# Pilot means behind part of the next tile, the last attention output unit split ahead, and Hyena splits behind the spectrum products

## The chip, the core and the metric

The kernel runs on one NeuronCore of one Trainium2 chip. The number that is compared is the device time of one launch in microseconds (us), the median of several runs. A core has engines that run side by side, each with its own queue of instructions: TensorE (PE, matrix products into the banks of PSUM), VectorE (DVE), ScalarE (ACT), GpSimd (POOL), and SyncE (SP), which issues the DMA transfers. They wait for each other through semaphores. TensorE works at one of two clock levels, 1.2 and 2.4 GHz; the profile gives the granted clock as a share of the higher one.

## What is computed

A backbone of two layers on 256 latent tokens of 1024 features, with 256 context tokens that only layer 0's first half-step and its attention read. Each layer is a half-step SwiGLU, a token mixer and another half-step SwiGLU. Layer 0's mixer is differential attention, layer 1's is a Hyena long convolution. Each of the six sub-layers is modulated by the conditioning and followed by a layer norm over the residual:

```python
def half_ffn(x, shift, scale, gate, wi, wo, g, b, alpha):
    y = swiglu(modulate(x, shift, scale), wi, wo)       # (silu(a) * u) @ wo, a and u from h @ wi
    return layer_norm(alpha * x + 0.5 * gate * y, g, b)

def bidir_long_conv(u, h_f, h_b, d_skip):
    ...
    uf = jnp.fft.rfft(u.astype(jnp.float32), n=n, axis=1)
    hf = jnp.fft.rfft(h_full, n=n, axis=0)
    y = jnp.fft.irfft(uf * hf[None], n=n, axis=1)[:, :L]
    return (y + u.astype(jnp.float32) * d_skip.astype(jnp.float32)).astype(u.dtype)

# layer i:
xl = half_ffn(xl, ml[0], ml[1], ml[2], ffa_wi[i], ffa_wo[i], ln_g[i, 0], ln_b[i, 0], alpha)
# mixer: diff_attention (i = 0) or hyena (i = 1), which is (x0 * bidir_long_conv(x1 * v, h_f, h_b, d_skip)) @ w_o
xl = layer_norm(alpha * xl + ml[5] * yl, ln_g[i, 1], ln_b[i, 1])
xl = half_ffn(xl, ml[6], ml[7], ml[8], ffb_wi[i], ffb_wo[i], ln_g[i, 2], ln_b[i, 2], alpha)
```

All of it is fp32. The FFT is done as products with tables.

## The kernel before

**Tiles.** Activations lie with features on the 128 partitions: eight tiles R[0] to R[7] of 128x256 for the latent tokens (named zl in the trace), and in the first, wide stage eight tiles Z of 128x512 (z) for latent and context together. An fp32 product is made of three products of high and low parts, so each weight is split: ScalarE casts the loaded weight (raw) to its high part (wH, line 237), and VectorE subtracts that from raw to get the low part (wL, line 238).

**Weights.** A queue `st` (class Stream) brings units of up to 1 MB in the order of use. Two raw buffers hold loaded units, three buffers hold split ones. `st.get` takes the next split unit, `st.done` gives its buffer back, and in the same call the next loaded unit's split is issued, and the next load. `st.spare(1)` allows one further unit to be split into four 512-column blocks (xwH, xwL) while the three buffers are taken; `st.spare(0)` ends that.

**Stages, in time.** The wide feed-forward (`ffn_wide`), attention over four pairs of heads with its output in four weight units of two tiles each (`Project`), three feed-forward stages (`ffn`, layer 0's second, layer 1's first, and, after Hyena, layer 1's second), and Hyena. A feed-forward stage's output has eight tiles j; tile j takes two weight units h = 0, 1 of 11 blocks each, a 512-column and a 256-column product per block, into one PSUM bank py. Then scalar_tensor_tensor on VectorE adds gate times py into R[j] (line 885 in the wide stage, 1202 in Project, 1255 in ffn).

**The norm and its pilot.** `Norm` takes the statistics while the output is still made. As soon as tile 0 is added, `pilot` makes the mean of tile 0 over its features on TensorE (lnpm, line 334 through the helper mm), and VectorE subtracts it from all eight tiles (line 735). This keeps the sums small. `add` takes the square on ScalarE and running sums on VectorE for each further tile, and `finish` closes the norm.

**Hyena.** `ramp` runs 12 units n of input weights, the first two interleaved; a unit is 48 products of 256 columns into a bank pxv. Behind unit n, `end` does the short convolution on ScalarE and VectorE (the product of both parts is pkeep), transposes tile n - 2 (ptr, then the halves pTh and pTl), and behind n = 6 and n = 10 (SPECTRUM) calls `spectrum`: products with a table into banks uf, and on VectorE 13 products and sums with the filter's spectrum (lines 1327 to 1334), whose halves yh and yl ScalarE and GpSimd make. After unit 11 follow the inverse transform (yt, 96 products) and a Project with four units.

**Order.** The code names instructions with priorities; a scheduler puts each engine's instructions into one fixed order, by priority and data dependencies. An engine runs its own list in that order. `tc.high_priority` moves what stands in it ahead, `tc.issue_after` puts instructions behind a given one. Splits are issued with a lowered priority. The lines that the change touches are tile_done and pilot, the loops over j in the three kinds of output, the last round (t == 3) of attention, and ramp and spectrum.

## Time and profile before

| | |
|---|---|
| median of 3 runs | 1368.24 us (1368.17 to 1372.35) |
| profiled execution | 1370.3 us, of which the span is 1368.1 |
| mean granted clock of TensorE | 0.976 |
| busy: TensorE, VectorE, ScalarE, GpSimd | 1312.9 us (96%), 1037.2 (76%), 660.0 (48%), 12.3 (1%) |
| DMA | 261.38 MB, mean 191 GB/s |

Times in rows are microseconds from the start of the span. A row of a timeline has start, duration, engine, line, operation, output<-inputs, and in square brackets how long the engine stood idle before it and what ended that. TensorE's products are pipelined, so the distance of two starts is what one costs, not the duration in its row. A product that is written x2 stands for two in a row. A row of windows has the stretch, its length, and then the busy time (with the number of instructions) of TensorE, its weight loads, VectorE, ScalarE and GpSimd, the granted clock, the DMA share and GB/s. In the profiled execution the wide output's second half runs around 360 to 390, attention's output ends at 628, the pilots of the three later feed-forward stages stand at 769, 967 and 1301, and Hyena's spectrum products around 1087 and, the second group, after unit 10.

### The profile page before, as it was taken

The numbers are of one execution on the slowest core, as the hardware profiler recorded it, in microseconds if no ns is written. First come the engines' busy times: TensorE is split into PE (matmuls) and PEld (weight loads), VectorE is DVE, ScalarE is ACT, GpSimd is POOL, SyncE is SP. The second block draws the span as 40 slices with busy tenths as digits, with TensorE's granted clock in tenths as the row PEclk, the third lists the DMA queues.
The fourth block names the chain that finished last, engine by engine and source line by source line (L and its number), as shares of the span: only waits on it lengthen the run. The fifth ranks groups of instructions, "written<-read, shape, count | busy, mean of one in ns | idle before, by whom it ended". The sixth has DMA issues, their size and how long they took to land.

```text
span 1368.1 us, 19280 instructions
## 1 busy us (share of the span) xinstructions
PE 1312.9 (96%) x7424; PEld 1129.7 (83%) x7424; DVE 1037.2 (76%) x1919; ACT 660.0 (48%) x1175; POOL 12.3 (1%) x12
## 2 busy tenths in 40 slices
PE   7999999999999999998999999999999889999997
PEld 4688888888788788887888888888899889888886
DVE  3899988889876777768777667766668789766665
ACT  1443322222233866655765446655446354666543
POOL 0000000000000000000000000000000020000000
PEclk9999999999999999998999999999999999999998
DMA  8967788878842212203654454554563523355452
GB/s 283 398 243 262 275 331 335 331 310 333 309 142 77 93 63 92 93 32 101 216 204 169 160 198 146 197 187 170 194 213 141 192 101 124 126 185 191 160 180 84
DMA packets 44419, 261.38 MB, mean 191 GB/s; under 512 B 4965, under 2 KB 6693, under 8 KB 19625
## 3 DMA queue, kind: packets, MB, share of 16 engines
q1 hardware_dynamic: 44328, 260.16, 53.0%
q8 instruction: 58, 0.95, 0.3%
q14 instruction: 33, 0.26, 0.1%
HBM read 256.99 MB, written 3.15 MB: 190 GB/s over the span
## 4 chain that ended last, share of the span: by engine, by line
PE 84%; DVE 9%; ACT 4%; issue 2%; DMA 1%; ACTq 0%; SPq 0%; DVEq 0%
PE py L334 24%; PE pa L334 22%; PE pu L334 22%; PE pxv L334 5%; PE pv L334 2%; DVE wL L238 1%; ACT wH L237 1%; PE hsp L334 1%; PE pka L334 1%; PE pkb L334 1%; PE warm L334 1%; DMA raw<-wia 1%; PE lnst L334 1%; PE po L334 1%; ACT rsw L925 1%
## 5 line engine op out<-in xcount | busy, mean ns | idle before, releaser
L238 DVE TENSOR_TENSOR wL<-raw,wH 128x1024 fp32r<-128x1024 f32 (+1 forms) x358 | 389.9, 1108 | 119.6 <-ACT wH L237 116.9
L237 ACT CAST wH<-raw 128x1024 fp32r<-128x1024 f32 (+1 forms) x358 | 331.0, 956 | 217.4 <-PE py L334 122.6
L334 PE MATMUL pa<-xhl,wH 128*128 128x512 f32 x520 | 188.2, 399 | 5.6 <-DVE xhl L811 5.6
L334 PE MATMUL py<-g,wH 128*128 128x512 f32 (+1 forms) x594 | 188.1, 374 | 0.0
L334 PE MATMUL pu<-xhl,wH 128*128 128x512 f32 x520 | 187.9, 398 | 0.0
L489 DVE SCALAR_TENSOR_TENSOR rawa<-rawa,condb 128x1024 f32<-128x1024 f32 x128 | 151.2, 1220 | 3.5 <-DMA rawa<-adr 3.3
L334 PE MATMUL py<-g,wL 128*128 128x256 f32 x528 | 148.9, 282 | 0.0
L334 PE MATMUL pa<-xhl,wL 128*128 128x256 f32 x520 | 146.5, 282 | 0.0
L334 PE MATMUL pu<-xhl,wL 128*128 128x256 f32 x520 | 146.3, 281 | 0.0
L334 PEld LDWEIGHTS py<-g,wH 128*128 128x128 f32 x594 | 107.9, 189 | 21.0
L334 PEld LDWEIGHTS pa<-xhl,wH 128*128 128x128 f32 x520 | 98.6, 190 | 29.3 <-DVE xhl L811 4.1
L334 PEld LDWEIGHTS pu<-xhl,wH 128*128 128x128 f32 x520 | 98.7, 190 | 23.2
L334 PEld LDWEIGHTS py<-g,wL 128*128 128x128 f32 x528 | 100.6, 191 | 0.1
L334 PEld LDWEIGHTS pa<-xhl,wL 128*128 128x128 f32 x520 | 99.2, 191 | 0.1
L334 PEld LDWEIGHTS pu<-xhl,wL 128*128 128x128 f32 x520 | 99.3, 191 | 0.0
L841 ACT ACTIVATE sil<-pa 128x512 f32<-128x512 f32 x22 | 13.2, 598 | 152.6 <-PE pa L334 152.6
L334 PE MATMUL pxv<-xhl,wH 128*128 128x256 f32 x384 | 75.5, 298 | 5.2 <-DVE pTl L508 3.8
L334 PEld LDWEIGHTS pxv<-xhl,wH 128*128 128x128 f32 x384 | 64.4, 205 | 5.9 <-DVE pTl L508 4.1
L334 PE MATMUL pa<-xh,wH 128*128 128x512 f32 x176 | 68.6, 390 | 0.0
L334 PE MATMUL pa<-xh,wL 128*128 128x512 f32 x176 | 68.5, 389 | 0.0
L334 PE MATMUL pu<-xh,wH 128*128 128x512 f32 x176 | 68.5, 389 | 0.0
L334 PE MATMUL pu<-xh,wL 128*128 128x512 f32 x176 | 68.5, 389 | 0.0
(314 smaller groups left out, 2601.2 us busy)
## 6 DMA issues: line engine op xcount, KB each, us to landing
rawa<-adr SPq DMA_DIRECT2D x64, 1024.0 KB, 6.9
raw<-wia SPq DMA_DIRECT2D x44, 1024.0 KB, 4.8
raw<-wib SPq DMA_DIRECT2D x44, 1024.0 KB, 4.8
raw<-woa SPq DMA_DIRECT2D x32, 704.0 KB, 4.1
raw<-wob SPq DMA_DIRECT2D x32, 704.0 KB, 4.1
rawa<-adx SPq DMA_DIRECT2D x8, 1024.0 KB, 10.1
raw<-wqk SPq DMA_DIRECT2D x8, 1024.0 KB, 4.7
raw<-whv SPq DMA_DIRECT2D x8, 1024.0 KB, 4.7
```

Of the source, the lines that this page charges most:

```text
L237: nc.scalar.copy(h[:, d], it["raw"][:, s:e])
L238: nc.vector.tensor_tensor(lo[:, d], it["raw"][:, s:e], h[:, d].bitcast(F32), OP.subtract)
L334: return nc.tensor.matmul(o, l, r, start=start, stop=stop, skip_group_check=True)
L489: V.scalar_tensor_tensor(junk if q else w, w, 1.0, condb[:, q, :], OP.mult, OP.mult, accum_out=mod[i][:, q, 2 * u + h:2 * u + h + 1])
L841: S.activation(s, pa, AF.Silu)
L925: S.copy(s3[32 * b:32 * b + 32], ps[32 * (b ^ 1):32 * (b ^ 1) + 32])
```

## The change

Three edits.

(a) The pilot moves. `tile_done` and `pilot` take an instruction `after`, and the pilot's product is issued behind it. In the wide stage it comes behind the first ES = 5 of 11 blocks (15 of 33 products) of tile 1, in ffn behind tile 1's first unit (22 products), in Project behind part of tile 2's products, where tile 0 and tile 1 are both reported. The eight subtracts follow the pilot.

(b) In attention's last round `st.spare(1)` stands ahead of the round and `st.spare(0)` behind it, so one of the output's weight units may be split into blocks.

(c) In Hyena, for n = 6 and n = 10, `end` (convolution, transposition, spectrum) runs first, and `st.done`, with the split that it issues, is put behind the last VectorE instruction of the spectrum products, which are now in a function `product` of their own, unchanged.

```diff
@@ -719,18 +719,20 @@
         def __init__(self, z, n):
             self.z, self.n = z, n
 
-        def tile_done(self, j):
+        def tile_done(self, j, after=None):
 
             with tc.high_priority(120):
                 if j == 0:
-                    self.pilot()
+                    self.pilot(after)
                 if j < KT - 1:
                     self.add(j)
 
-        def pilot(self):
+        def pilot(self, after):
+
             z, n = self.z, self.n
             ps = bank("lnpm")[:, :n]
-            mm(ps, opil, z[0], True, True)
+            with tc.issue_after(after.ins):
+                mm(ps, opil, z[0], True, True)
             for t in range(KT):
                 V.tensor_tensor(z[t], z[t], ps, OP.subtract)
 
@@ -876,6 +878,8 @@
                 mid = gemm(o, G, NH, 0, ES)
                 if half == 1 and j == KT - 1:
                     nrm.early(mid)
+                if half == 1 and j == 1:
+                    nrm.tile_done(0, mid)
                 gemm(o, G, NH, ES)
                 st.done(it, half == 1 and j == KT - 1)
                 wide_side(100 + 50 * half + j)
@@ -884,7 +888,7 @@
                         c = slice(T * q, T * q + T)
                         pin(V.scalar_tensor_tensor(Z[j][:, c], py[:, c], g[:, q, j:j + 1], Z[j][:, c], OP.mult,
                                                    OP.add), j if half else 0)
-                if half == 1:
+                if half == 1 and j:
                     nrm.tile_done(j)
         return nrm
 
@@ -1154,6 +1158,7 @@
                 main = v
             else:
                 pj = Project(O, gate_cols(0, 5, 1, False))
+                st.spare(1)
 
                 def pj_parts():
                     pj.open(2)
@@ -1165,6 +1170,7 @@
 
                 thread(main, PLAN_LAST, now)
                 thread(pj_parts(), PLAN_LAST, now, KT)
+                st.spare(0)
         return pj.close(6)
 
     class Project:
@@ -1195,13 +1201,17 @@
                     mid = gemm(outs[o:o + 1], self.O, KT, k0, ks) if ks > k0 else None
                     if j == KT - 1:
                         self.nrm.early(mid)
-                    gemm(outs[o:o + 1], self.O, KT, ks)
+                    last = gemm(outs[o:o + 1], self.O, KT, ks)
+                    if j == 2:
+                        self.nrm.tile_done(0, mid or last)
+                        self.nrm.tile_done(1)
                     if o:
                         st.done(it, j == KT - 1)
                     with tc.high_priority(PJP):
                         pin(V.scalar_tensor_tensor(R[j], py[:, T * o:T * o + T], self.gt[:, 0, j:j + 1], R[j],
                                                    OP.mult, OP.add), j)
-                    self.nrm.tile_done(j)
+                    if j > 1:
+                        self.nrm.tile_done(j)
                 self.jj += 1
             return self.nrm
 
@@ -1249,15 +1259,19 @@
                     mid = mm(py[:, :T], wl, g[:, :T], False, last)
                 if j == KT - 1 and h == 0:
                     nrm.early(mid)
+                if j == 1 and h == 0:
+                    nrm.tile_done(0, mid)
                 st.done(it, j == KT - 1 and h == 1)
             with tc.high_priority(PJP):
                 for n in range(1 if alone else 2):
                     pin(V.scalar_tensor_tensor(R[j], py[:, T * n:T * n + T], gt[:, 0, j:j + 1], R[j], OP.mult, OP.add), j)
             ada_side(ADA_FFN[s + str(i)].count(NF + j))
-            nrm.tile_done(j)
+            if j:
+                nrm.tile_done(j)
         return nrm
 
-    def ramp(unit, gemm, X, end, n, first=2, ks=5):
+    def ramp(unit, gemm, X, end, n, late=(), first=2, ks=5):
+
 
         grp = [unit() for _ in range(first)]
         gemm([o for g in grp for o in g[2]], X, KT, 0, ks)
@@ -1268,8 +1282,12 @@
             else:
                 it, pp, outs = unit()
                 gemm(outs, X, KT)
-            st.done(it)
-            end(pp, f)
+            if f in late:
+                with tc.issue_after(end(pp, f).ins):
+                    st.done(it)
+            else:
+                st.done(it)
+                end(pp, f)
 
 
     def split_table(src, name):
@@ -1322,21 +1340,27 @@
                         mm(ps, au[tt][0][:, c], lo, False, False)
                         mm(ps, au[tt][1][:, c], h, False, tt == 1)
                     U[ft] = ps
-                ur, ui, hr, hi = U[f], U[2 + f], sp[f, dh], sp[2 + f, dh]
-                yr, yi, t1, t2 = blk("yr"), blk("yi"), blk("yt1"), blk("yt2")
-                V.tensor_tensor(yr, ur, hr, OP.mult)
-                V.tensor_tensor(t1, ui, hi, OP.mult)
-                V.tensor_tensor(yr, yr, t1, OP.subtract)
-                V.tensor_tensor(yi, ur, hi, OP.mult)
-                V.tensor_tensor(t2, ui, hr, OP.mult)
-                V.tensor_tensor(yi, yi, t2, OP.add)
-                if f == 0:
-                    V.tensor_tensor(yi[0:1, :], ui[0:1, :], nyq[dh][0:1, :], OP.mult)
-                for ft, y in ((f, yr), (2 + f, yi)):
-                    h, lo = blk("yh", F32R), blk("yl", F32R)
-                    S.copy(h, y)
-                    nc.gpsimd.tensor_tensor(lo, y, h.bitcast(F32), OP.subtract)
-                    YH[ft, dh], YL[ft, dh] = h, lo
+                last = product(f, dh, U[f], U[2 + f])
+            return last
+
+        def product(f, dh, ur, ui):
+
+            hr, hi = sp[f, dh], sp[2 + f, dh]
+            yr, yi, t1, t2 = blk("yr"), blk("yi"), blk("yt1"), blk("yt2")
+            V.tensor_tensor(yr, ur, hr, OP.mult)
+            V.tensor_tensor(t1, ui, hi, OP.mult)
+            V.tensor_tensor(yr, yr, t1, OP.subtract)
+            V.tensor_tensor(yi, ur, hi, OP.mult)
+            V.tensor_tensor(t2, ui, hr, OP.mult)
+            last = V.tensor_tensor(yi, yi, t2, OP.add)
+            if f == 0:
+                last = V.tensor_tensor(yi[0:1, :], ui[0:1, :], nyq[dh][0:1, :], OP.mult)
+            for ft, y in ((f, yr), (2 + f, yi)):
+                h, lo = blk("yh", F32R), blk("yl", F32R)
+                S.copy(h, y)
+                nc.gpsimd.tensor_tensor(lo, y, h.bitcast(F32), OP.subtract)
+                YH[ft, dh], YL[ft, dh] = h, lo
+            return last
 
         def unit():
             it = st.get("w")
@@ -1369,9 +1393,9 @@
             if 0 <= n - LAG < KT:
                 transposed(n - LAG)
             if n in SPECTRUM:
-                spectrum(SPECTRUM.index(n))
-
-        ramp(unit, gemm, [(x[:, :T], x[:, T:]) for x in X], end, 12)
+                return spectrum(SPECTRUM.index(n))
+
+        ramp(unit, gemm, [(x[:, :T], x[:, T:]) for x in X], end, 12, SPECTRUM)
         O = []
         for j in range(KT):
             dh, c = j // 4, slice(P * (j % 4), P * (j % 4) + P)
```

How the instructions stand. On VectorE in layer 0's second feed-forward stage around the pilot's subtracts (zl are the tiles, lnpm the pilot's bank, wL the low parts of weights, py the output banks), before:

```order
857 L1255 SCALAR_TENSOR_TENSOR zl_3030<-py_6617,gate08_6615,zl_3030 128x256 x2
858 L238 TENSOR_TENSOR wL_6671<-raw_6603,wH_6670 128x704
859 L735 TENSOR_TENSOR zl_3030<-zl_3030,lnpm_6680 128x256 x2
860 L735 TENSOR_TENSOR zl_3031<-zl_3031,lnpm_6680 128x256 x2
861 L735 TENSOR_TENSOR zl_3032<-zl_3032,lnpm_6680 128x256 x2
862 L735 TENSOR_TENSOR zl_3033<-zl_3033,lnpm_6680 128x256 x2
863 L238 TENSOR_TENSOR wL_6671<-raw_6603,wH_6670 128x704
864 L238 TENSOR_TENSOR wL_6717<-raw_6646,wH_6716 128x704 x2
865 L1255 SCALAR_TENSOR_TENSOR zl_3030<-py_6693,gate08_6615,zl_3030 128x256 x2
866 L745 TENSOR_TENSOR lnd_6690<-zl_3030 128x256
```

and in the changed kernel:

```order
862 L1267 SCALAR_TENSOR_TENSOR zl_3030<-py_6627,gate08_6625,zl_3030 128x256 x2
863 L238 TENSOR_TENSOR wL_6681<-raw_6613,wH_6680 128x704 x2
864 L737 TENSOR_TENSOR zl_3030<-zl_3030,lnpm_6713 128x256 x2
865 L737 TENSOR_TENSOR zl_3031<-zl_3031,lnpm_6713 128x256 x2
866 L737 TENSOR_TENSOR zl_3032<-zl_3032,lnpm_6713 128x256 x2
867 L737 TENSOR_TENSOR zl_3033<-zl_3033,lnpm_6713 128x256 x2
868 L238 TENSOR_TENSOR wL_6727<-raw_6656,wH_6726 128x704
869 L1267 SCALAR_TENSOR_TENSOR zl_3030<-py_6690,gate08_6625,zl_3030 128x256
870 L238 TENSOR_TENSOR wL_6727<-raw_6656,wH_6726 128x704
871 L1267 SCALAR_TENSOR_TENSOR zl_3030<-py_6690,gate08_6625,zl_3030 128x256
872 L238 TENSOR_TENSOR wL_6757<-raw_6686,wH_6756 128x704
873 L747 TENSOR_TENSOR lnd_6723<-zl_3030 128x256
```

The eight subtracts have moved behind one whole weight split (wL_6681, both halves, before wL_6671 with one half on either side), and the additions of tile 1 follow them with one half of the next split in front of each.

On ScalarE at the end of attention (prob are the softmax's exponentials, oh the normalised output of a pair of heads, lnq and lnsq the norm's squares, wH the weights' high parts), before:

```order
331 L507 CAST oh_5155<-ob_5047 128x256
332 L507 CAST oh_5159<-ob_5099 128x256
333 L741 ACTIVATE lnq_5192<-zl_3030 128x256
334 L237 CAST wH_5200<-raw_4710 128x1024 x2
335 L744 ACTIVATE lnsq_5209<-zl_3030 128x256
336 L744 ACTIVATE lnsq_5220<-zl_3031 128x256
337 L237 CAST wH_5230<-raw_4951 128x1024 x2
338 L744 ACTIVATE lnsq_5239<-zl_3031 128x256
```

and in the changed kernel the same unit, raw_4710, is cast here:

```order
313 L1058 ACTIVATE prob_4906,sums_4904<-sc_4895,mx_4903 128x512
314 L1058 ACTIVATE prob_4909,sums_4904<-sc_4896,mx_4903 128x512
315 L1058 ACTIVATE prob_4940,sums_4938<-sc_4929,mx_4937 128x512
316 L237 CAST wH_4963<-raw_4710 128x1024
317 L1058 ACTIVATE prob_4943,sums_4938<-sc_4930,mx_4937 128x512
318 L507 CAST vh_4971<-pv_4766 128x512
319 L237 CAST wH_4963<-raw_4710 128x1024
320 L507 CAST vh_4975<-pv_4767 128x512
```

The cast of that unit, both halves, which stood behind the norm's first square (lnq), stands among the last exponentials.

On VectorE in Hyena around the first spectrum products (yr, yi, yt1, yt2 are the products, uf the transformed banks, spec the filter's spectrum, pTl the low halves of transposed tiles), before:

```order
1184 L1364 TENSOR_TENSOR pkeep_9123<-cv_9617 128x256
1185 L238 TENSOR_TENSOR wL_9751<-raw_9533,wH_9750 128x1024
1186 L508 TENSOR_TENSOR pTl_9626<-ptr_9629,pTh_9625 128x128
1187 L508 TENSOR_TENSOR pTl_9626<-ptr_9766,pTh_9625 128x128
1188 L238 TENSOR_TENSOR wL_9751<-raw_9533,wH_9750 128x1024
1189 L508 TENSOR_TENSOR pTl_9628<-ptr_9629,pTh_9627 128x128
1190 L1327 TENSOR_TENSOR yr_9650<-uf_9636,spec_8443 128x512
1191 L1328 TENSOR_TENSOR yt1_9652<-uf_9643,spec_8447 128x512
1192 L1330 TENSOR_TENSOR yi_9651<-uf_9636,spec_8447 128x512
1193 L1329 TENSOR_TENSOR yr_9650<-yr_9650,yt1_9652 128x512
1194 L1331 TENSOR_TENSOR yt2_9653<-uf_9643,spec_8443 128x512
1195 L508 TENSOR_TENSOR pTl_9628<-ptr_9766,pTh_9627 128x128
```

and in the changed kernel the end of these products:

```order
1203 L1357 TENSOR_TENSOR yi_9653<-uf_9645,nyq_8461 1x512
1204 L508 TENSOR_TENSOR pTl_9630<-ptr_9776,pTh_9629 128x128
1205 L1350 TENSOR_TENSOR yr_9685<-uf_9671,spec_8455 128x512
1206 L1351 TENSOR_TENSOR yt1_9687<-uf_9678,spec_8459 128x512
1207 L1353 TENSOR_TENSOR yi_9686<-uf_9671,spec_8459 128x512
1208 L1352 TENSOR_TENSOR yr_9685<-yr_9685,yt1_9687 128x512
1209 L1354 TENSOR_TENSOR yt2_9688<-uf_9678,spec_8455 128x512
1210 L1355 TENSOR_TENSOR yi_9686<-yi_9686,yt2_9688 128x512
1211 L508 TENSOR_TENSOR pTl_9628<-ptr_9846,pTh_9627 128x128
1212 L238 TENSOR_TENSOR wL_9704<-raw_9471,wH_9703 128x1024
1213 L1319 SCALAR_TENSOR_TENSOR cv_9768<-pxv_9711,vec_84,cv_9768 128x255
1214 L1319 SCALAR_TENSOR_TENSOR x0keep_9134<-pxv_9783,vec_84,x0keep_9134 128x255
```

The split that stood ahead of the first spectrum product (wL_9751) is not there any more; instead the first half of an earlier unit's split (wL_9704, from raw_9471, which is raw_9461 before) stands behind the last one.

## Rows read from the trace of the kernel before

**Rows 1.** The page, parts 1 and 4: busy time, last chain

```profile
PE 1312.9 (96%) x7424; PEld 1129.7 (83%) x7424; DVE 1037.2 (76%) x1919; ACT 660.0 (48%) x1175; POOL 12.3 (1%) x12
...
PE 84%; DVE 9%; ACT 4%; issue 2%; DMA 1%; ACTq 0%; SPq 0%; DVEq 0%
```

**Rows 2.** TensorE's waits: line, releaser, total us, times, longest

```profile
PE ptr L1350 <- DVE pkeep L1364: 4.4, 1, 4.4
PE lnpm L334 <- DVE zl L1255: 4.3, 3, 1.9
PE pxv L334 <- DVE pTl L508: 3.8, 1, 3.8
PE py L334 <- DVE zl L1202: 3.7, 4, 1.2
...
PE lnpm L334 <- DVE z L885: 1.6, 1, 1.6
...
PE py L334 <- ACT wH L237: 0.9, 1, 0.9
```

**Rows 3.** Timeline of TensorE, layer 1's last feed-forward stage, at the pilot

```profile
1299.52 0.39 PE L334 MATMUL py<-g,wH 128*128 128x512 f32 x1
...
1299.86 0.40 PE L334 MATMUL py<-g,wH 128*128 128x512 f32 x1
...
1301.56 0.67 PE L334 MATMUL lnpm<-zl,opil 128*128 128x256 f32 x2 [1.19 <-DVE zl L1255]
```

**Rows 4.** Timeline of TensorE, the wide stage, at the pilot

```profile
365.49 0.39 PE L334 MATMUL py<-gl,wH 128*128 128x512 f32 x1
365.71 0.39 PE L334 MATMUL py<-gh,wL 128*128 128x512 f32 x1
367.65 1.13 PE L334 MATMUL lnpm<-z,opil 128*128 128x512 f32 x2 [1.55 <-DVE z L885]
```

**Rows 5.** Timeline of TensorE, layer 1's first feed-forward stage, at the pilot

```profile
964.70 0.28 PE L334 MATMUL py<-g,wL 128*128 128x256 f32 x1
966.92 0.67 PE L334 MATMUL lnpm<-zl,opil 128*128 128x256 f32 x2 [1.94 <-DVE zl L1255]
```

**Rows 6.** Timeline of VectorE, layer 1's last feed-forward stage, behind the pilot

```profile
1302.30 2.73 DVE L735 TENSOR_TENSOR zl<-zl,lnpm 128x256 f32<-128x256 f32 x8
...
1306.83 1.69 DVE L238 TENSOR_TENSOR wL<-raw,wH 128x704 fp32r<-128x704 f32 x2 [0.99 <-ACT wH L237]
```

**Rows 7.** Timeline of ScalarE, attention's output

```profile
613.29 1.98 ACT L237 CAST wH<-raw 128x1024 fp32r<-128x1024 f32 x2
```

**Rows 8.** Windows: stretch, us, busy (instructions) of each engine, granted clock, DMA share

```profile
612.06:627.84 15.78, 12.09 (x71) 11.07 (x70) 13.84 (x30) 6.77 (x12) 0.00 (x0) 0.78 0.19 67
968.00:971.00 3.00, 3.00 (x11) 2.52 (x11) 3.00 (x10) 0.62 (x1) 0.00 (x0) 0.50 0.92 334
1083.68:1114.07 30.39, 22.18 (x149) 21.98 (x150) 24.58 (x42) 13.71 (x27) 6.62 (x4) 0.83 0.34 122
```

**Rows 9.** Timeline of VectorE, attention's last softmax and its output

```profile
592.12 0.67 DVE L508 TENSOR_TENSOR vl<-pv,vh 128x512 fp32r<-128x512 f32 x1
...
615.11 0.87 DVE L1202 SCALAR_TENSOR_TENSOR zl<-py,gate,zl 128x256 f32<-128x256 f32 x2
```

**Rows 10.** Timeline of ScalarE, Hyena, a weight cast

```profile
1083.42 1.04 ACT L237 CAST wH<-raw 128x1024 fp32r<-128x1024 f32 x1 [6.47 <-PE pxv L334]
```

**Rows 11.** Timeline of VectorE, Hyena, around the first spectrum products

```profile
1084.50 1.22 DVE L238 TENSOR_TENSOR wL<-raw,wH 128x1024 fp32r<-128x1024 f32 x1 [6.05 <-ACT wH L237]
...
1090.56 0.68 DVE L1332 TENSOR_TENSOR yi<-yi,yt 128x512 f32<-128x512 f32 x1
...
1097.12 1.79 DVE L1332 TENSOR_TENSOR yi<-yi,yt 128x512 f32<-128x512 f32 x1
...
1100.28 0.48 DVE L1301 SCALAR_TENSOR_TENSOR cv<-pxv,vec,cv 128x255 f32<-128x255 f32 x1
...
1104.82 0.41 DVE L1364 TENSOR_TENSOR pkeep<-cv 128x256 f32<-128x256 f32 x1
```

## Prediction

> **What bounds the kernel now.** I read four views in this order. The page's first and fourth parts show where the end is set: TensorE is busy for 96% of the span and carries 84% of the chain that ended last [rows 1]. So nothing on another engine pays unless TensorE waits for it, and a gain can come from two things only: time in which TensorE stands still, and time in which it works at the lower of its two clock levels. The list of TensorE's waits is therefore read next. Three kinds of wait in it belong to the lines of this change [rows 2]: the pilot (lnpm) waits for the first normalised tile, 4.3 us in three feed-forward stages and 1.6 us in the wide one; the attention output (py) waits 3.7 us for R tiles on VectorE and 0.9 us for a weight cast on ScalarE; Hyena waits 3.8 us for a transposed tile (pTl) and 4.4 us for pkeep. That is 18.7 us in all. The third view is the timeline around each of these waits, and the fourth is windows, which add the granted clock behind them.
>
> **Pilots.** Before, TensorE runs the pilot as soon as tile 0 ends, so it waits until VectorE has added tile 0 into the residual. After, the pilot stands behind part of tile 1's products, which need no pilot. No instruction is added; the pilot and its eight subtracts are the same.
> In layer 1's last feed-forward stage the products follow each other in pairs 0.34 to 0.35 us apart. The pair after 1299.86 was due at 1300.21, and the pilot starts at 1301.56 [rows 3]: 1.35 us is lost, and the pilot's own time stays. Layer 0's second feed-forward stage has the same wait (4.3 us in three, less 1.9, leaves 1.2 for each of the two), so 1.35 again. In the wide stage the step is 0.22 us, so the next product was due at 365.94, and the pilot comes at 367.65 [rows 4]: 1.7 us.
> In layer 1's first feed-forward stage the next pair was due at 964.82 (0.12 behind 964.70) and the pilot comes at 966.92 [rows 5]: 2.1 us. Behind this longer stop the granted clock is 0.50 from 968 to 971, that is the 1.2 GHz level [rows 8]; three microseconds at half speed cost 1.5 more. So this pilot costs 3.6.
> Together 1.7 + 1.35 + 1.35 + 3.6 = 8.0 us.
> What is late next? The eight subtracts hold VectorE for 2.73 us [rows 6] and now start inside tile 1. The weight subtract behind them is for a unit that TensorE reaches a whole unit (22 products, 3.8 us) later, and before, VectorE stands idle 0.99 us at that place, waiting for the cast [rows 6]. The tile's own addition moves back behind the subtracts, but another accumulator bank is free. I take nothing for it. If this cover is gone, each pilot gives back at most its own 1.35 to 1.7, and the 3.6 keeps only its clock part: 8.0 falls to about 2.
>
> **Attention output.** From the product behind the pilot at 612.06 to the end of this output at 627.84 are 15.78 us, with 71 products and a mean clock of 0.78 [rows 8]. A 256-column product takes 0.12 at the full level (a pair of 0.345 less the 0.22 to 0.23 of a 512-column one [rows 3, 4]), so 71 need 8.5 us, and 7.3 us are lost there to waits and to the clock. The first cause is the fourth weight unit's cast, 1.98 us long, which ScalarE starts only at 613.29 [rows 7], behind the first square of the norm; the second is the eight subtracts, behind which the additions at 615.11 [rows 9] stand.
> After, the third unit is split early into spare blocks, so the fourth finds a normal buffer and both are ready ahead of this stretch: the 0.9 us wait goes. The pilot stands behind part of tile 2. Left is the wait for the bank that tile 2's addition frees: 2.73 of subtracts, up to 1.98 of casts in front of the norm's square, and 0.87 of additions, partly side by side, against 24 products (2.9 us) that cover them. That lies between 0 and 2.7; I take 1.3, and 0.4 for the next one.
> New on the queues, earlier, are four 512-column casts on ScalarE and four subtracts on VectorE, which now stand among the exponentials and the maxima of the last softmax. Nearest is the 0.67 us of a 128x512 subtract [rows 9]: four are 2.7 us if none is hidden, and nothing if all are. The last scores are also no longer issued alternately. The place has other work, so I take 1.0.
> Sum: 7.3 - 1.3 - 0.4 - 1.0 = 4.6 us; bounds 7.3 and, with 2.7 + 0.4 + 2.7 and another 2.3 at the lower clock, -0.8.
>
> **Hyena.** Before, ScalarE's cast of unit 10's weights waits 6.47 us for TensorE to leave unit 7 [rows 10]. VectorE's half of that split stands at the head of its queue from 1078.45 to 1084.50, idle for 6.05 us [rows 11], with the spectrum products behind it although their inputs are there. Banks come free late, and TensorE first waits 3.8, then 4.4 us [rows 2]. From 1083.68 to 1114.07 it has 149 products in 30.39 us, is busy for 22.18 and has a mean clock of 0.83 [rows 8]: 8.2 us idle, and against 149 x 0.125 = 18.6 another 3.6 lost to the clock, 11.8 together.
> After, the products come first and VectorE fills its 6 us, so unit 8 starts at once and ends near 1089.5. But the split that now stands behind the products is unit 9's, the next one. Thirteen products of up to 0.68 each [rows 11], with a stop near 1082 to 1085 for the same cast, end near 1090.3. Then come the first half of unit 9's subtract (1.2), the convolutions of unit 8 and pkeep, a table's subtract (0.6), and only then the second half. In the trace the chain from the first convolution's addition at 1100.28 to the end of pkeep at 1105.2 takes 4.9 us [rows 11]; with a wait for ScalarE's part that puts the second half near 98.1. TensorE can run about 12 products (1.5 us) in between, so it stands 98.1 - 89.5 - 1.5 = 7.1 us. With one fall of the clock in place of two (2.5 in place of 3.6), 9.6 us are lost where 11.8 were: 2.2 us gained. The bounds are +5 (the second half comes with the first) and -3 (each of the four SBUF subtracts takes as long as the slow one below, and the clock stays low for as long as before).
> A row speaks against this part. The same operation, yi<-yi,yt, takes 0.68 us at 1090.56 and 1.79 at 1097.12 [rows 11], in a stretch in which GpSimd is busy for 6.62 us with four subtracts [rows 8]. The Trainium skill, SBUF — State Buffer, section "Who interferes with whom", has a rule for it: a VectorE instruction with two SBUF inputs and a GpSimd one that reads SBUF share one read interface, and whoever comes second is blocked for the whole instruction. The trace agrees with its 1.79. By the rule the weight subtracts that now stand directly behind the products meet GpSimd's subtracts too; two of them at 1.1 us more each would leave the Hyena part at 0 and the sum at 12.6. By the row alone one such meeting was there before and one is there after, which is what the sum has.
>
> **The sum.** 8.0 + 4.6 + 2.2 = 14.8 us. The profiled execution took 1370.3 us (span 1368.1), so it would be 1355.5; the median of the runs shown is 1368.24, 2.1 lower, so I forecast **1353 us**. A difference of 0.3% is 4.1 us, about what a measurement of this kernel can tell from no change.
>
> **Rivals.**
> 1. *Hyena's stall only moves and grows.* Unit 9's split behind the products keeps TensorE idle for longer than the two old waits. For it: its two halves stand 12 queue rows apart. Against it: VectorE's idle 6.05 us is really freed. At -3 the sum is 9.6: 1358.6 us. Chance 0.20.
> 2. *The attention output gains nothing.* The split ahead delays the softmax by its 2.7, and the wait behind the subtracts again brings the clock to 0.50. At -0.8 the sum is 9.4: 1358.8 us. Against it: the cast that opens this stretch of waits is gone. Chance 0.16.
> 3. *The pilots' waits only move* onto the additions or the next weights, so that 2 of 8.0 remains: 1359.4 us, and with rival 1 or 2 as well, 1364.7, no change. For it: VectorE works 76% of the span. Against it: the idle time in rows 6. Chance 0.12, half of it no change.
> 4. *The clock stays low in Hyena; slower.* The one stall is longer (7.1 against 3.8 and 4.4), and 12 scattered products do not end it. For it: the two old stalls brought the low level too, at 3.6 us. If it lasts through units 9 to 11, their 43 + 48 + 48 products (16.7 us) take twice that, and the gain is used up: from there on the kernel is slower than before. Through the inverse transform too (96 products, 11.5 us) it is 28.2 - 14.8 = 13 us slower, 1382 us. Against it: after both old stalls the full level returned, or the mean of the stretch would not be 0.83. [...] Chance 0.05.
>
> **How the numbers follow.** The forecast (a gain of 11 to 20) has 0.47, rivals 0.20, 0.16, 0.12 and 0.05. The best sum, 8.0 + 7.3 + 5 = 20.3, gives 1347.9; a little for a pilot that also ends other waits, 1346. At the other end 1362 takes in rivals 1, 2 and half of 3. Faster by over 0.3%: 0.47 + 0.20 + 0.16 + 0.06 = 0.89; within: 0.06; slower: 0.05.
>
> **What would show it.** In the changed kernel's waits, lnpm should be gone and no new wait for zl above 1.5 us should be there; the stretch from 968 to 971 should have a clock of 1.00. The 0.9 us wait for a cast in the attention output should be gone, and from the pilot to that output's end should be about 11 us in place of 16. In Hyena no VectorE wait of 6 us should stand ahead of the products; a single TensorE stop near 1090 to 1098, in that kernel's time some 10 us earlier, should take the place of 3.8 and 4.4. The forecast is wrong if a second stop stands behind it, or if the clock is still 0.50 ten microseconds later.

## The result and the profile after

The changed kernel takes 1355.24 us (median of 4 runs, 1350.86 to 1357.97) against 1368.2 (1367.93 to 1372.35): ratio 0.9895, 95% interval 0.9861 to 0.9929, about 14 us faster. On another chip it took 1361.04 against 1371.34, ratio 0.9919 (0.9891 to 0.9947), 11 us faster. The forecast was 1353 us, a gain of 14.8.

The page of the profiled execution (1356.75 us, span 1355.0), busy time and the last chain; they answer to [rows 1]:

```profile
PE 1310.6 (97%) x7424; PEld 1127.2 (83%) x7424; DVE 1035.4 (76%) x1921; ACT 660.5 (49%) x1177; POOL 12.7 (1%) x12
...
PE 87%; DVE 7%; ACT 3%; DMA 1%; issue 1%; ACTq 0%; SPq 0%
```

TensorE's busy time is nearly the same, its idle time 11 us smaller. Its waits, in answer to [rows 2]:

```profile
PE ptr L1374 <- DVE pkeep L1388: 3.2, 1, 3.2
...
PE pxv L334 <- DVE wL L238: 2.7, 1, 2.7
...
PE py L334 <- DVE zl L1211: 2.0, 3, 1.1
PE at L1080 <- ACT prob L1058: 1.7, 1, 1.7
...
PE lndl L334 <- DVE lnd L747: 1.0, 1, 1.0
```

All lnpm waits and the cast wait at py are gone. Hyena's two waits have other causes and are 2.3 us shorter together, the zl waits of py 1.7. New are 1.7 us for prob in attention's last softmax and 1.0 for lnd.

**The pilots.** TensorE's timeline around the pilot in layer 1's last feed-forward stage, in answer to [rows 3]:

```profile
1291.38 0.27 PE L334 MATMUL py<-g,wL 128*128 128x256 f32 x1
1291.49 0.59 PE L334 MATMUL lnpm<-zl,opil 128*128 128x256 f32 x2
1291.74 0.58 PE L334 MATMUL py<-g,wH 128*128 128x512 f32 x1
```

The pilot starts 0.11 us behind the last product, with no wait. In layer 1's first feed-forward stage the clock no longer falls behind it (a window in answer to the second row of [rows 8]; the columns are the same):

```profile
962.00:966.00 4.00, 4.00 (x24) 3.48 (x23) 3.15 (x8) 2.00 (x3) 0.00 (x0) 1.00 0.62 205
```

To compare the kernels stage by stage I take the time from one norm's lnrb to the next, and inside a feed-forward output the time from its first product to tile 7's first, less its 154 pairs at the spacing measured ahead of the pilot and behind it (347 or 353 ns; the last section has more on these two). In the wide stage it is the time from the first to the last of the second half's 264 products, 62.34 before and 60.51 after, less 263 steps of 0.2267. What remains is what the pilot costs, its own two products included (0.25 us, in the wide stage 0.46):

| stage (us) | before, stage | after, stage | before, cost of pilot | after |
|---|---|---|---|---|
| wide, to its end | 427.48 | 425.98 | 2.7 | 0.9 |
| attention | 206.08 | 203.94 | | |
| layer 0, second | 194.26 | 192.50 | 1.85 | 0.43 |
| layer 1, first | 199.09 | 195.25 | 4.12 | 0.43 |
| Hyena | 139.41 | 135.44 | | |
| layer 1, second | 192.83 | 192.89 | 1.87 | 0.42 |

**Attention** from the last key product (pka, pkb) to lnrb has three stretches: to the last orb (the first of its two products; the softmax and values) 35.49 before and 37.04 after; to the last output product 20.06 and 14.63; to lnrb 5.84 and 6.15. The wait for prob, 1.7 us, accounts for the longer first stretch. The output's first half behind the pilot now runs without a stop, two short waits are left, and the granted clock, 0.78 behind the pilot before [rows 8], is 1.00 throughout (the window has TensorE alone: busy, clock, DMA share, GB/s):

```profile
613.25 0.70 PE L334 MATMUL lnpm<-zl,opil 128*128 128x256 f32 x2
...
618.96 0.50 PE L334 MATMUL py<-oh,wH 128*128 128x256 f32 x2 [1.08 <-DVE zl L1211]
...
620.91 0.50 PE L334 MATMUL py<-oh,wH 128*128 128x256 f32 x2 [0.26 <-DVE zl L1211]
...
609.14:623.77 14.63, 13.05 (x96) 1.00 0.00 0
```

**Hyena** from its start to unit 11's last product takes 98.10 us before and 93.97 after; its projection with the norm 29.79 and 29.95. VectorE behind the spectrum products, in answer to [rows 11] (the last product, unit 9's first half, the first addition of unit 8's convolutions, pkeep, unit 9's second half):

```profile
1080.35 0.69 DVE L1355 TENSOR_TENSOR yi<-yi,yt 128x512 f32<-128x512 f32 x1
...
1081.16 2.09 DVE L238 TENSOR_TENSOR wL<-raw,wH 128x1024 fp32r<-128x1024 f32 x1
1083.17 0.47 DVE L1319 SCALAR_TENSOR_TENSOR cv<-pxv,vec,cv 128x255 f32<-128x255 f32 x1
...
1086.70 0.41 DVE L1388 TENSOR_TENSOR pkeep<-cv 128x256 f32<-128x256 f32 x1
...
1087.63 1.22 DVE L238 TENSOR_TENSOR wL<-raw,wH 128x1024 fp32r<-128x1024 f32 x1
```

GpSimd's last two subtracts, beside which unit 9's first half runs:

```profile
1080.45 1.72 POOL L1361 TENSOR_TENSOR yl<-yr,yh 128x512 fp32r<-128x512 f32 x1 [1.55 <-ACT yh L1360]
1082.13 2.26 POOL L1361 TENSOR_TENSOR yl<-yi,yh 128x512 fp32r<-128x512 f32 x1
```

and TensorE over these stretches (windows, columns as above):

```profile
1079.00:1082.00 3.00, 1.62 (x14) 1.42 (x12) 2.96 (x6) 1.75 (x5) 1.55 (x1) 1.00 0.29 87
1082.00:1085.00 3.00, 0.62 (x3) 0.42 (x3) 3.00 (x6) 1.38 (x4) 2.39 (x2) 0.98 0.00 0
1085.00:1088.00 3.00, 0.83 (x4) 0.82 (x4) 2.96 (x8) 1.10 (x4) 0.00 (x0) 0.50 0.00 0
1088.00:1091.00 3.00, 3.00 (x13) 2.55 (x12) 3.00 (x6) 0.94 (x3) 0.00 (x0) 0.50 0.35 82
1091.00:1094.00 3.00, 3.00 (x24) 3.00 (x24) 1.12 (x1) 0.39 (x1) 0.00 (x0) 0.88 0.94 314
```

Unit 8 runs without a stop up to 1080; then 2.7 and 3.2 us of waiting, 0.50 in the clock from 1085 to 1091, and the full level from 1094.

### The profile page after: what moved, and what is told of

It reads as the page before. It is cut to its first block, busy times and chain, and to the rows that moved or that the text cites. A ratio compares the mean times of both kernels' runs of the same rounds, so it can differ in the third digit from the quotient of the medians.

```text
span 1355.0 us, 19282 instructions
## 1 busy us (share of the span) xinstructions
PE 1310.6 (97%) x7424; PEld 1127.2 (83%) x7424; DVE 1035.4 (76%) x1921; ACT 660.5 (49%) x1177; POOL 12.7 (1%) x12
## 4 chain that ended last, share of the span: by engine, by line
PE 87%; DVE 7%; ACT 3%; DMA 1%; issue 1%; ACTq 0%; SPq 0%
PE py L334 24%; PE pa L334 23%; PE pu L334 23%; PE pxv L334 5%; PE pv L334 2%; DVE wL L238 2%; ACT wH L237 1%; PE hsp L334 1%; PE pka L334 1%; PE pkb L334 1%; PE warm L334 1%; PE uf L334 1%; PE lnst L334 1%; DMA raw<-wia 1%; PE po L334 1%
## 5 line engine op out<-in xcount | busy, mean ns | idle before, releaser
L334 PE MATMUL pu<-xl,wH 128*128 128x512 f32 x176 | 68.5, 389 | 0.0
L334 PE MATMUL pa<-xl,wH 128*128 128x512 f32 x176 | 68.5, 389 | 0.0
```

Of the source, the lines that this page charges most:

```text
L334: return nc.tensor.matmul(o, l, r, start=start, stop=stop, skip_group_check=True)
```

## The experiments

Each stands against the kernel before on the same chip; TensorE's stretches are taken as above.

**The three parts alone.** Each is the kernel before with some lines of the diff shown ahead: for pilots those of tile_done, pilot and the three outputs; for hyena those of ramp, spectrum, product and end; for attn these:

```diff
                 pj = Project(O, gate_cols(0, 5, 1, False))
+                st.spare(1)
...
                 thread(pj_parts(), PLAN_LAST, now, KT)
+                st.spare(0)
```

> Only the moved pilots (wide, three feed-forward stages, both output projections). Theory (the gain is the sum of local waits): the four lnpm waits (4.3 + 1.6 us) go, and with the half clock behind the one near 967 the kernel is 7 to 8 us faster than before, near 1360.5. Rival (the waits only move onto the additions or the next weights): 2 us faster or less, with new py waits of over 1 us in the feed-forward stages. Second rival (the spacing of TensorE's products, 347 or 353 ns for a pair, changes by chance from run to run and hides the local gain): lnpm waits are gone but a stage's length differs by up to 1 us for 55 us of products at the other spacing.

> Only the spare unit in attention's last round. Theory: the 0.9 us cast wait at the output's end goes, but the eight subtracts still stand ahead of tile 2's addition, and the last softmax comes 1.7 us later: about -1 to +1.5 us gained, near 1368, so most of the attention gain needs the moved pilot too. Rival (the cast was the cause of the whole stretch of waits): 3 us or more faster, near 1365.

> Only Hyena's splits behind the spectrum products. Theory: stops of 3.8 and 4.4 us become stops of about 2.7 (unit 9's weights) and 3.2 (pkeep), one fall of the clock less; 4 to 5 us faster, near 1363.7. Rival (the stall only moves): within 1 us of before, 1367 to 1369.

Pilots alone: 1362.3 against 1369.3, ratio 0.9937 (0.9910 to 0.9963), 8.6 us faster by the ratio and 7.0 by the medians. In the three later feed-forward stages the pilot costs 0.42, 0.43 and 0.43 us, as in the changed kernel, and no new wait is in these stages: the rival that the waits only move falls. In attention, where the pilot moved too, the output still takes 20.41 us (the first row's two waits are attention's; of the second row's two one is attention's, 0.9, and one Hyena's):

```profile
PE py L334 <- DVE zl L1209: 3.3, 2, 2.6
...
PE py L334 <- ACT wH L237: 1.6, 2, 0.9
```

Attention alone: 0.9980 (0.9955 to 1.0004), unclear in time; in the trace the output takes 14.12 us, the stretch before it 38.56 (3.1 more than before), lnrb comes after 5.41; from the last key product on 58.09 in place of 61.39, 3.3 us less. So the late cast was the cause of the whole stretch of waits, as the rival had it, and the theory, which shared it with the pilot, falls. The waits (of the first row 1.1 is attention's), and the window behind the one for prob (TensorE alone):

```profile
PE py L334 <- DVE zl L1204: 2.0, 2, 1.1
PE at L1076 <- ACT prob L1054: 1.7, 1, 1.7
...
589.00:592.00 3.00, 3.00 (x18) 0.54 0.00 0
```

Here the granted clock falls behind the wait for prob, and in the changed kernel, which has the same stop of 1.68 us there, it stays at 1.00. That is why the early split costs this stretch 3.1 us here and 1.6 there. The run next below has the stop, the fall and the longer stretch (38.58), again, lag3 and yldve have the stop alone (37.04).

Hyena alone: 0.9985 (0.9958 to 1.0012), unclear in time; in the trace 95.60 us to unit 11's end where before has 98.10, the stops are 2.69 and 2.85, and the projection takes 30.58 in place of 29.79. The stage is 1.7 us shorter, less than the expected 4 to 5. The clock has a part in this: windows of the stage's first 15 us and from there to unit 11's end (columns as above), of the changed kernel

```profile
1017.67:1032.67 15.00, 13.68 (x98) 13.28 (x99) 13.29 (x36) 11.03 (x20) 0.00 (x0) 0.89 0.09 28
1032.67:1111.64 78.97, 73.04 (x547) 70.34 (x547) 65.77 (x115) 39.57 (x67) 9.13 (x6) 0.96 0.47 166
```

and of the run hyena:

```profile
1027.74:1042.74 15.00, 13.85 (x89) 13.48 (x90) 13.06 (x35) 10.21 (x18) 0.00 (x0) 0.77 0.10 29
1042.74:1123.34 80.60, 75.06 (x556) 72.28 (x555) 65.94 (x115) 40.31 (x68) 9.13 (x6) 0.94 0.45 163
```

The kernel before has 0.89 and 0.94. With the pilots alone Hyena's stage is 137.54, 1.9 shorter (1.3 of it in the projection, which takes 28.44). The two do not simply add: in the changed kernel the projection takes 29.95, no less than before, so the 4.0 us that the stage gains lie ahead of unit 11's end.

**Which split stands behind the products?** 

```diff
-            if f in late:
-                with tc.issue_after(end(pp, f).ins):
+            if f - 1 in late:
+                with tc.issue_after(last.ins):
                     st.done(it)
             else:
                 st.done(it)
-                end(pp, f)
+            last = end(pp, f)
```

> The changed kernel, but the release that is put behind the spectrum products is that of the unit after (7 and 11), so unit 9's split stays where it was before and unit 10's goes behind the products. Theory (the two remaining stops, 2.7 and 3.2 us, come from unit 9's split standing behind the products): both go, with the half clock behind them; 5 to 8 us faster than the changed kernel, near 1348 to 1350. Rival (the stops come from the convolutions and pkeep, which stand behind the products in any case): the pkeep stop of about 3 us stays, 1 to 3 us faster, near 1353.

1355.61 us, ratio 0.9904 (0.9873 to 0.9935), near the changed kernel's on the two other chips (0.9895 and 0.9919). Unit 9's split is early again, but two stops stay; the VectorE rows are unit 10's split, in two halves, and pkeep:

```profile
PE ptr L1374 <- DVE pkeep L1388: 3.8, 1, 3.8
...
PE pxv L334 <- DVE pTl L508: 2.6, 1, 2.6
...
1085.41 2.05 DVE L238 TENSOR_TENSOR wL<-raw,wH 128x1024 fp32r<-128x1024 f32 x1
...
1088.94 1.22 DVE L238 TENSOR_TENSOR wL<-raw,wH 128x1024 fp32r<-128x1024 f32 x1
...
1091.64 0.41 DVE L1388 TENSOR_TENSOR pkeep<-cv 128x256 f32<-128x256 f32 x1
```

The theory falls: the pkeep stop is there without unit 9's split. That it comes from unit 8's convolutions, as the rival has it, this run alone does not show, since both halves of unit 10's split now stand between the products and pkeep. The run yldve below bears it out: there no weight split stands between them, and the stop for pkeep stays.

**The same kernel once more.**

> The changed kernel once more, unaltered. Theory (the spacing of TensorE's product pairs, 347 or 353 ns, is taken up by chance at stops and pilots): in this execution at least one of the three later feed-forward stages has another spacing than in the first profile (347, 353, then 347 up to the pilot and 353 behind it), and its length differs by about 2.6 us ahead of the pilot and 1 us behind it. Rival (the spacing follows from the program): the same spacings in every stage.

The theory holds. TensorE's timeline among the input products of layer 1's first feed-forward stage, 97 us from its start, the first execution:

```profile
919.70 0.40 PE L334 MATMUL pa<-xhl,wH 128*128 128x512 f32 x1
...
920.05 0.40 PE L334 MATMUL pa<-xhl,wH 128*128 128x512 f32 x1
...
920.41 0.40 PE L334 MATMUL pu<-xhl,wH 128*128 128x512 f32 x1
```

and the second one, of the same program:

```profile
929.62 0.39 PE L334 MATMUL pu<-xhl,wH 128*128 128x512 f32 x1
...
929.97 0.39 PE L334 MATMUL pu<-xhl,wH 128*128 128x512 f32 x1
...
930.31 0.39 PE L334 MATMUL pu<-xhl,wH 128*128 128x512 f32 x1
```

A pair takes 353 ns in the one (0.35, 0.36) and 347 in the other (0.35, 0.34; the means over 5 us are 353 to 354 and 346 to 347), at a granted clock of 1.00 in both. The stage takes 195.25 and 191.40 us. Layer 0's second goes the other way, 192.50 and 195.63, and layer 1's second 192.89 and 195.37. The wide stage differs by more, 425.98 and 433.54; already its first 45 us (window of TensorE alone: busy, clock, DMA share, GB/s) differ, after:

```profile
0.00:45.00 45.00, 37.20 (x186) 0.89 0.93 313
```

and again:

```profile
0.00:45.00 45.00, 34.94 (x155) 0.79 0.92 314
```

**A later place for the spare unit.**

```diff
                 pj = Project(O, gate_cols(0, 5, 1, False))
-                st.spare(1)
...
                 thread(main, PLAN_LAST, now)
+                st.spare(1)
                 thread(pj_parts(), PLAN_LAST, now, KT)
```

> The changed kernel, but the spare unit is allowed only behind attention's last scores, so that the third unit is split into a normal buffer and the fourth into spare blocks behind the softmax. Theory (the 2 to 3 us that the stretch from the last key product to the output's first half got longer come from the split among the maxima): that stretch is 35.5 us as before, the wait of 1.7 us for prob is gone, and the output still takes 14 to 15 us in place of 20; 2 us faster than the changed kernel. Rival (the fourth unit is then late again): a cast or wL wait of about 1 us at the output, and no gain.

1353.64 us, ratio 0.9876 (0.9847 to 0.9904); in time this is not clear of the changed kernel on this chip (0.9891 to 0.9947). In the trace the stretch with the softmax is 35.59 us, the wait for prob is gone, the output takes 14.62. There the theory holds: the early split among the maxima cost 1.5 us, and 3 where the clock fell behind its wait.

**Transpositions one unit later.**

```diff
-LAG = 2
+LAG = 3
```

> The changed kernel with LAG = 3: each tile is transposed one unit later. Theory (the second stop of 3.2 us is a transposition whose pkeep stands behind the products): with a unit more of time that stop shrinks to under 1.5 us or goes; 2 to 4 us faster than the changed kernel. Rival (the spectrum products then begin later, since their last transposed tile comes later, and all behind them moves): a stop of 4 us or more at the next unit's weights, no gain or slower.

1353.03 us, ratio 0.9876 (0.9849 to 0.9903), in time not clear of the changed kernel either. In the trace both stops are gone; the stretch of the products and the one behind it:

```profile
1073.00:1083.00 10.00, 10.00 (x85) 9.96 (x84) 9.90 (x16) 4.65 (x8) 3.19 (x2) 1.00 0.01 2
1083.00:1093.00 10.00, 9.64 (x79) 9.31 (x78) 9.20 (x20) 5.64 (x15) 4.09 (x3) 1.00 0.43 157
```

TensorE is idle for 0.4 us in 20, where the changed kernel is idle for 5.9 in ten. To unit 11's end the stage takes 88.22 us (93.97 in the changed kernel), but the projection 34.03 (29.95), with waits of 2.0 for zl and 2.9 for lndg. So 4.1 of 5.8 us are given back; the stage is 1.7 shorter. That VectorE's late weight splits do it is seen only in so far as they stand in front of these additions; no run takes them away.

**The low halves on VectorE.**

```diff
-                nc.gpsimd.tensor_tensor(lo, y, h.bitcast(F32), OP.subtract)
+                V.tensor_tensor(lo, y, h.bitcast(F32), OP.subtract)
```

> The changed kernel with the spectrum's low halves subtracted on VectorE in place of GpSimd (eight subtracts of about 0.7 us more on VectorE). Theory (a VectorE subtract with two SBUF inputs is held up by GpSimd): the weight subtract behind the products takes 1.2 in place of 2.1 us, no yi takes over 0.75; but VectorE has 2.8 us more ahead of unit 9's second half, so the two stops of TensorE together grow by 1 to 2 us. Rival (the long subtract has another cause): it still takes about 2 us.

1357.2 us, ratio 0.9899 (0.9874 to 0.9925). Without GpSimd beside it the weight subtract of unit 9 takes what it takes elsewhere (pkeep, and the two halves):

```profile
1086.15 0.41 DVE L1388 TENSOR_TENSOR pkeep<-cv 128x256 f32<-128x256 f32 x1
...
1087.08 1.22 DVE L238 TENSOR_TENSOR wL<-raw,wH 128x1024 fp32r<-128x1024 f32 x1
...
1088.42 1.22 DVE L238 TENSOR_TENSOR wL<-raw,wH 128x1024 fp32r<-128x1024 f32 x1
```

TensorE's stops become one in place of 2.69 and 3.24, 5.93 together:

```profile
1086.62 0.69 PE L1374 MATMUL ptr<-ident,pkeep 128*128 128x128 f32 x2 [6.93 <-DVE pkeep L1388]
```

The expected times hold. But the order has changed as well: unit 9's first half stands behind pkeep here, so the run does not weigh the held-up subtract against four more operations on VectorE. What it shows is that pkeep is late with no weight split ahead of it: between the products and pkeep stand unit 8's convolutions, from 1082.62 on, and two of the moved subtracts (1.4 us).

**Together.** The later spare unit and LAG = 3; and the same with attention's pilot back at tile 0 (Project gets an argument `at`, 0 in attention and 2 in Hyena):

```diff
-                    if j == 2:
+                    if j == 2 == self.at:
                         self.nrm.tile_done(0, mid or last)
                         self.nrm.tile_done(1)
...
-                    if j > 1:
-                        self.nrm.tile_done(j)
+                    if j >= self.at:
+                        self.nrm.tile_done(j, last)
```

> The changed kernel with the spare unit allowed behind the last scores and LAG = 3 together. Theory (the two gains lie in stages far apart and add): attention's stretch from the last key product to the norm is 56 to 57 us, Hyena's 133 to 134 us from norm to norm; 3 us less than the changed kernel, some 1.4% less than before. Rival (another split order in attention moves what Hyena finds): one of the two stages is as long as in the changed kernel.

> As the run both, but in attention's output the pilot stands at tile 0 again, as before the change. Theory (with all four units split ahead the moved pilot has nothing left to hide in attention, and the norm's end is 0.7 us later for it): the output takes 14 to 15 us, the finish 5.4 in place of 6.15 us. Rival (the moved pilot does carry a part of the output's gain): the output takes 16 us or more, with a wait for zl of over 1.5 us behind the pilot.

1351.27 us, ratio 0.9851 (0.9829 to 0.9872), and 1350.21, ratio 0.9844 (0.9822 to 0.9867): on this chip, where before takes 1372.38, the second is 21 us faster than before, and the intervals of both lie below that of the changed kernel on the same chip (0.9891 to 0.9947). Attention from the last key product on takes 56.39 and 55.14 us (57.82 in the changed kernel), Hyena 133.04 and 132.61. With the pilot at tile 0 the output takes 14.12 us and lnrb comes after 5.42 in place of 6.15. Both theories hold.

## Why the forecast was right, and which terms were not

- *Feed-forward and wide pilots, 8.0.* Right in mechanism and size: 1.8, 1.4, 3.7 and 1.5, together 8.4. The trace of one execution hides the last: layer 1's second stage is no shorter, 192.83 and 192.89, because its pairs take 353 ns behind the pilot where before they took 347, and its first products ran longer at the low clock (0.79 over its first 16 us, 0.89 before). The 3.6 depends on the clock: in the runs attn and hyena, whose pilots stand as before, the same pilot waits 2.05 us, the granted clock stays at 1.00, and it costs 2.7 in place of 4.1.
- *Attention, 4.6.* From the last key product on it gained 3.6 (57.82 against 61.39). The output gained 5.4 in place of 5.6; the waits left at py are 1.08 and 0.26, against 1.3 and 0.4. The mis-sized term is "I take 1.0" for the split among the softmax: 1.6 here and 3.1 in attn. The norm's end, 0.3 later than before, had no term. The wrong step is "the second is the eight subtracts": the pilots moved alone leave the output at 20.41, and the split alone brings 14.12. The late cast set the time, and beside the split the moved pilot makes the output 0.5 longer and the norm's end 0.7 later. Of the 3.7 us of waits for R tiles in [rows 2] 0.9 belong to Hyena's projection; the sum did not use them.
- *Hyena, 2.2.* The order was as foretold: products first, unit 8 without a stop, then unit 9's half split and pkeep. But by the prediction's own sign this part failed: it named a second stop as a sign of being wrong, and a stop of 3.2 us stands behind the one of 2.7. Its working, with 12 products between the two halves, already had two. The terms were mis-sized: TensorE is idle for 5.9 us against 7.1. The chain from the first convolution's addition to the end of pkeep takes 3.9 (1083.17 to 1087.11) where the 4.9 of [rows 11] held a weight subtract as well, and no wait for ScalarE stands in it; the first half took 0.9 more. The low clock lasts 6.8 us (0.50 from 1085 to 1091 and its edges) where the mean of 0.83 over 30.39 us [rows 8] is 10.3, which is worth 1.7 against the 1.1 of the sum. The 2.3 us less of idle time and these 1.7 are the 4.0 that the stage gained. For the projection's moved pilot the sum had nothing, and the projection is no shorter (29.79 and 29.95).
- *The Trainium skill,* SBUF — State Buffer, section "Who interferes with whom": one weight subtract behind the products took 2.09 us; it began inside GpSimd's subtract of 1080.45 to 1082.17, as the rule has it. The second half, behind GpSimd's last subtract, and both halves in yldve took 1.22. It met one, not two, as the row had it; the sum stood.
- *Rival 1* falls (the stops are 5.9 against 8.2), *rival 2* in its sign (attention gains 3.6), *rival 3* (each pilot gave back 1.4 to 3.7 and no new wait stands in its place), and *rival 4*: the full level is back by 1094, 7 us behind the last stop.
- The local terms sum to 16.0 (8.4 + 3.6 + 4.0) where the forecast had 14.8: attention came out 1.0 lower and Hyena 1.8 higher, which in part cancel. The two spans differ by 13.1. The rest lies where nothing was changed: attention's head is 1.4 us longer in the execution after, and layer 1's second stage hides its 1.5. That the median lies 2 us from the forecast is in part luck: the four executions scatter over 7 us, and on the other chip the gain was 11.

## What to carry to other kernels

Put a small product that waits for another engine behind work of the same engine that needs nothing; where its wait was the only cost it goes whole, and where another wait ended last (attention's cast) moving it does nothing. When a split or a load is moved off one stretch, price the queue in which it lands: among short dependent operations it cost 1.5 us, or 3 where the clock fell behind the new wait, and one step later nothing. When a block of work is put ahead in an in-order queue, look at everything behind it that TensorE needs next: of Hyena's two stops neither went without another in its place until the transpositions came a unit later, and then 4.1 of the 5.8 us came back in the projection.

## What was not expected of the hardware

At a granted clock of 1.00, a pair of a 512- and a 256-column product takes 347 ns in some stretches and 353 in others. In the feed-forward stages it changed only at a stage's start or at a pilot, and in two executions of the same program it was different in three stages of three. A stage ahead of its output is 126.3 to 127.5 us long at the one and 128.4 to 129.8 at the other, the output 53.8 and 54.8. What sets it stays open.

The clock did not answer to the length of a stop alone. Behind the same stop of 1.68 us for prob it fell to 0.50, the 1.2 GHz level, in two executions (attn, next) and stayed at 1.00 in four (after, again, lag3, yldve); behind the pilot of layer 1's first stage it fell after a stop of 1.94 us (before) and stayed after 2.05 (attn, hyena).

With a wide stage that differs by 7.6 us between two executions, this is why the parts of this change, of 2 to 8 us, could be told in the trace by stretches and only in part in the times.
